# A hybrid encoder kernel: output weights in the order of use, and a spill buffer by half and head

## The chip, the cores and the metric

The kernel runs on one core of one Trainium2 chip. The metric is the device time of one execution in microseconds. Three timed runs of the kernel before lie between 4213.9 and 4220.34 us, with a median of 4215.14 us.

## The reference, cut to what matters

Two sequences (1024 and 2048 tokens, 1024 channels, f32) go through two layers with shared weights. The even layer projects the normed input, runs a state-space mixer (S5, 512 channels) beside a bidirectional RWKV-7 mixer (8 heads of 64 channels), gates both, and puts the concatenation through one output projection. The odd layer is windowed attention with 16 heads of 64, a gate, and an output projection. What the change touches is this:

```python
y = ((y - mean) * lax.rsqrt(var + RW_LN_EPS)).reshape(B, L, RW_WIDTH)   # per head
y = y * rw_ln_g + rw_ln_b
bonus = jnp.sum(rh * kh * rw_r_k, axis=-1, keepdims=True) * vh          # (B, L, 8, 64)
yb = (y + bonus.reshape(B, L, RW_WIDTH)) * jax.nn.silu(z_rw)
x = x + jnp.concatenate([ya, yb], axis=-1) @ ev_w_out                   # 1024 x 1024
...
x = x + (o * jax.nn.silu(z)) @ od_w_out                                 # 1024 x 1024
```

## The kernel before, in words

The program runs in four parts, one after the other. Part one makes S5's inputs. Part two (`input_rkv` with `s5`) projects r, k, v and the low-rank inputs of RWKV and spills them to DRAM. Part three (`mixers`) runs the RWKV recurrence. Part four runs three phases: `even_out` (the even layer's output projection), `odd_in` (the odd layer's input projections) and `attention` (with the odd layer's output projection).

Parts one, two and four are recorded first and then put in order by a planner, class `Program`. `record` notes every operation with a modelled cost and the earlier operations that it depends on. `put` (L414) issues them greedily, by the modelled clocks of the engines and by rank. For a DMA the modelled cost is the bytes of its destination (L378), plus 0.48 us of SP for each issue (L452). A read of an input tensor makes no dependency (L393); a DRAM tile is compared by the address range that it covers (`box`, L343). Each engine then executes its instructions in that fixed order. All DMAs are issued by SP, on one queue. Since the planner replays the recorded operations, nearly every instruction of these parts carries L412 in the profile, so the tile names tell them apart.

RWKV's bonus: `input_rkv` handles the channels in four blocks p of 128 channels, two heads each. It works in segments of 512 tokens, two for the first sequence and four for the second. L820 stores each block's bonus `v` (128 channels on 128 partitions, some hundreds of tokens) into the DRAM tile `bon` of shape [4, 2, 64, L]: block, half, channel in the head, token. There are 24 such stores.

`even_out` works in tiles of 256, 256 and 512 tokens for the first sequence and four times 512 for the second. RWKV's heads are used there in another order: all second halves first, then all first halves. So block b of 128 rows is made of the same half of two neighbouring blocks p. L1810 loads the bonus for block b with the token range of the tile: two runs of 64 rows each. For a tile, `even_out` loads S5's and RWKV's results and gates, normalises RWKV rows (GpSimd, DVE, ScalarE), transposes them on TensorE, and for each b combines them with the bonus and the gate in two DVE operations (L1811, L1812). `emit` (L1769) then splits the block into a high part (ScalarE) and a low part (DVE). TensorE multiplies 8 blocks by the split weights, three products for each (L1724). The tiles `bo` for the bonus have two buffers, shared with a temporary of the normalisation.

The output weights are read by `load_rows` (L1704): eight row blocks of 128 rows, each loaded into a raw tile and split by ScalarE and DVE into a high and a low part. For the even layer (8 loads of 512 KB), the first four blocks are 128 neighbouring rows of `ev_w_out`. The last four follow the order of the heads: two runs of 64 rows (L1743). For the odd layer (`weights`, L1907) there are 8 loads of 256 KB for each of two halves of the columns. All of them are two runs of 64 rows (L1909). `weights(0)` comes at the start of `attention`, and the planner places it beside `odd_in`'s first tile. `weights(1)` comes with the first attention values.

Of the kernel before, what the change touches and what calls it, by code (L numbers as in the profile page):

```python
# [11 lines left out]
F32 = mybir.dt.float32  # L12
# [7 lines left out]
P = 128  # L20
D = 1024
# [449 lines left out]
class Kern:  # L471
# [134 lines left out]
    def spill_tiles(self, dp):  # L606
        self.sp = []
        for s, L in enumerate(self.L):
            t = {}
            t["rk"] = dp.tile([L // P, P, 4, 4, P], F32, name=f"rk{s}")  # L610
            t["v"] = [dp.tile([P, 512], F32, name=f"v{s}_{i}") for i in range(L // P)]
            t["tw"] = dp.tile([64, L], F32, name=f"tw{s}")
            t["bon"] = dp.tile([4, 2, 64, L], F32, name=f"bon{s}")
            t["s5"] = [dp.tile([4, P, 256], F32, name=f"s5{s}_{i}") for i in range(L // 256)]
            t["y"] = [[dp.tile([P, 512], F32, name=f"y{s}_{d}_{i}") for i in range(L // P)] for d in range(2)]
            t["h"] = [dp.tile([min(4, (L - g) // P), P, KT, P], F32, name=f"h{s}_{g}") for g in range(0, L, 512)]
            for n in ("zr", "zs"):
                t[n] = [dp.tile([P, 4, 4, P], F32, name=f"{n}{s}_{i}") for i in range(L // 512)]
            t["x1"] = [dp.tile([P, D], F32, name=f"x1{s}_{i}") for i in range(L // P)]
            t["qkv"] = [dp.tile([P, 2, 1536], F32, name=f"qkv{s}_{i}") for i in range(L // 256)]  # L620
            t["z"] = [dp.tile([P, 8, 512], F32, name=f"z{s}_{i}") for i in range(L // 512)]
            self.sp.append(t)

        nb = [L // 8 for L in self.L]
        self.col = [2, nb[0] + 6]
        for n in ("u", "ys"):
            x = [dp.tile([8, 16, 8, sum(nb) + 8], F32, name=f"{n}_{p}") for p in range(4)]
            for s, t in enumerate(self.sp):
                t[n] = [a[:, :, :, self.col[s]:self.col[s] + nb[s]] for a in x]
            setattr(self, n, x)  # L630
        self.strips = [dp.tile([16, 4, 31, 16], F32, name=f"strip{p}") for p in range(8)]

        self.wsp = [dp.tile([P, 2, KT, P], F32, name=f"wsp{i}") for i in range(13)]
# [64 lines left out]
    def input_rkv(self, st):  # L698
        nc, ins, tc = self.nc, self.ins, self.tc
        W = ins["ev_w_in"][0]  # L700
        cp = st.enter_context(tc.tile_pool(name="p1c", bufs=1))
# [29 lines left out]
        for s, L in enumerate(self.L):  # L731
            t = self.sp[s]
            for t0 in range(0, L, self.seg):
                T = min(self.seg, L - t0)
                last = t0 + T == L
                o0 = t0 - P if t0 else 0
                o1 = L if last else t0 + T - P
# [4 lines left out]
                h = self.stored_T(t["h"], t0, T)  # L742
# [28 lines left out]
                for p in range(4):  # L771
# [3 lines left out]
                    a = o1p.tile([P, SEGW], F32, name="a")[:, :w]  # L775
# [22 lines left out]
                    b = o1p.tile([P, SEGW], F32, name="sq")[:, :w]  # L798
# [4 lines left out]
                    r = o1p.tile([P, SEGW], F32, name="r")[:, :w]  # L803
# [6 lines left out]
                    v = o1p.tile([P, SEGW], F32, name="v")[:, :w]  # L810
# [5 lines left out]
                    for c, n in chunks:  # L816
                        pn = psx.tile([P, 512], F32, name="px")
                        nc.tensor.matmul(pn[:, :n], self.ones2, pb[:, c:c + n], start=True, stop=True)
                        nc.vector.tensor_tensor(v[:, c:c + n], pn[:, :n], v[:, c:c + n], MULT)
                    nc.sync.dma_start(t["bon"][p].rearrange("h r l -> (h r) l")[:, o0:o1], v)  # L820
                for i in range(nt):
                    nc.sync.dma_start(t["v"][o0 // P + i], vt[i])

# [913 lines left out]
    def even_out(self, st):  # L1737
        tc, nc, ins = self.tc, self.nc, self.ins
        cp = st.enter_context(tc.tile_pool(name="eoc", bufs=1))
        wo = ins["ev_w_out"][0]  # L1740

        turned_rows = lambda a: a.rearrange("(b h r) c -> h b r c", h=2, r=64)
        rows = [wo[P * k:P * k + P] for k in range(4)] + [turned_rows(wo[512:D])[1 - b // 2, 2 * (b % 2):2 * (b % 2) + 2] for b in range(4)]  # L1743
        ln = cp.tile([P, 8], F32, name="ln")
        nc.sync.dma_start(ln, ins["rwt_ln"])
        lng, lnb = ln[:, 0:4], ln[:, 4:8]
# [1 line left out]
        lp = st.enter_context(tc.tile_pool(name="eol", bufs=2))  # L1748
# [6 lines left out]
        for s, L in enumerate(self.L):  # L1755
            t = self.sp[s]
            sizes = [self.T1] * (512 // self.T1) if s == 0 else []
            sizes += [512] * (L // 512 - (s == 0))
            for t0, TT in zip(itertools.accumulate([0] + sizes), sizes):
# [9 lines left out]
                def emit(k, m):  # L1769
                    nc.scalar.activation(mh[k], m, AF.Copy)  # L1770
                    nc.vector.tensor_tensor(ml[k], m, f32(mh[k]), SUB)
# [33 lines left out]
                for b in range(4):  # L1805
                    pt = pst.tile([P, 512], F32, name="pt")[:, :TT]
                    for i, y in enumerate(yn):
                        nc.tensor.transpose(pt[:, i * P:(i + 1) * P], y[:, b * P:(b + 1) * P], self.ident)
                    bo = lp.tile([P, 512], F32, name="bo")[:, :TT]
                    nc.sync.dma_start(bo, t["bon"][2 * (b % 2):2 * (b % 2) + 2, 1 - b // 2, :, t0:t0 + TT])  # L1810
                    nc.vector.scalar_tensor_tensor(out=bo, in0=pt, scalar=lng[:, b:b + 1], in1=bo, op0=MULT, op1=ADD)  # L1811
                    nc.vector.scalar_tensor_tensor(out=bo.rearrange("c (i t) -> c i t", t=P), in0=bo.rearrange("c (i t) -> c i t", t=P), scalar=lnb[:, b:b + 1],  # L1812
                                                   in1=zr[:, :, b], op0=ADD, op1=MULT)
                    emit(4 + b, bo)
# [76 lines left out]
    def attention(self, st):  # L1891
        nc, ins, tc = self.nc, self.ins, self.tc
        V, Q = nc.vector, nc.gpsimd
        cp = st.enter_context(tc.tile_pool(name="atc", bufs=1))
# [5 lines left out]
        lp = st.enter_context(tc.tile_pool(name="atl", bufs=2))  # L1900
# [5 lines left out]
        psm = st.enter_context(tc.tile_pool(name="psm", bufs=self.B4, space=PSUM))  # L1906
        def weights(c):  # L1907

            v = ins["od_w_out"][0].rearrange("(k e g r) c -> k g e r c", e=2, g=4, r=64)  # L1909
            rows = [v[b // 4, b % 4] for b in range(8)]  # L1910
            return self.load_rows(cp, lp, [r[:, :, 512 * c:512 * c + 512] for r in rows], f"wo{c}", 0.5, (["wr"], 512, 2))

        w = [weights(0)]
        ring = itertools.cycle(range(16))

# [144 lines left out]
        for j, kv in turn + [(None, None)] * self.LAG:  # L2060
            if j is not None:
                if kv == self.KA and j and j + 2 < len(blocks):
                    keys(j + 2)
                if kv == self.QA and j + 1 < len(blocks):
                    qts[j + 1] = queries(j + 1)
                todo.append(scores(j, kv, qts[j]))
            if len(todo) > self.LAG or j is None:
                x = todo.popleft()
                values(*x)
                if len(w) < 2:  # L2070
                    w.append(weights(1))
                if outs and x[1] == self.OA:
                    d = outs.popleft()
                    out(d, made.pop(d))
                if x[1] == 3:
                    outs.append(x[0])
# [16 lines left out]
    def build(self):  # L2093
        tc = self.tc
        with ExitStack() as root:
# [11 lines left out]


_PLAIN = ["x_prompt", "x_sample", "ev_norm", "ev_w_in", "s5_log_dt", "s5_glu_w", "s5_glu_b", "rw_mu", "rw_w0",
          "rw_w_up", "rw_a0", "rw_a_up", "rw_k_k", "rw_k_a", "rw_r_k", "rw_ln_g", "rw_ln_b", "ev_w_out", "od_norm",  # L2110
          "od_w_in", "at_q_norm", "at_k_norm", "at_sink", "od_w_out"]


def _layout(inputs):
    import numpy as np

    a = {n: np.ascontiguousarray(inputs[n]) for n in _PLAIN}
    g = lambda n, axes, shape: np.ascontiguousarray(np.asarray(inputs[n])[0].transpose(axes).reshape(shape))

    a["ev_w_zr"] = np.ascontiguousarray(np.asarray(inputs["ev_w_in"])[0][:, ZR0:].reshape(D, 4, 2, 64)[:, :, ::-1].transpose(0, 2, 1, 3).reshape(D, 512))  # L2120

    a["od_w_z"] = np.ascontiguousarray(np.asarray(inputs["od_w_in"])[0][:, 1536:].reshape(D, 2, 2, 4, 64).transpose(0, 1, 3, 2, 4).reshape(D, 1024))
    ln = [np.asarray(inputs[n])[0].reshape(2, 2, 2, 64)[:, :, ::-1] for n in ("rw_ln_g", "rw_ln_b")]
    a["rwt_ln"] = np.ascontiguousarray(np.concatenate([x.transpose(1, 3, 2, 0).reshape(P, 4) for x in ln], axis=1))

    for n in ("a_re", "a_im"):
        a["s5t_" + n] = g("s5_" + n, (0, 2, 1), (128, 32))
    for n in ("b_re", "b_im"):
        a["s5t_" + n] = g("s5_" + n, (0, 2, 1, 3), (128, 32, 16))
    for n in ("c_re", "c_im"):  # L2130
        a["s5t_" + n] = g("s5_" + n, (0, 3, 1, 2), (128, 32, 16))
    a["s5t_d"] = np.ascontiguousarray(np.asarray(inputs["s5_d"])[0].reshape(32, 16).T)
    return a
# [14 lines left out]
```

## Time and profile before

| | us |
|---|---|
| median of 3 runs (lowest, highest) | 4215.14 (4213.9, 4220.34) |
| the profiled execution's own time | 4222.45 |
| its span in the trace | 4220.7 |
| TensorE (PE) busy, share of the span | 3795.9, 90% |
| VectorE (DVE) busy | 2819.6, 67% |
| ScalarE (ACT) busy | 1933.0, 46% |
| GpSimd (POOL) busy | 1611.2, 38% |
| mean granted TensorE clock | 0.952 |

The page cuts the span into 40 slices of 105.5 us. A digit is the busy share in tenths; PEclk is the granted TensorE clock in tenths of full speed. `even_out` begins in slice 22 (from 0) and ends in slice 25. There PE shows 6, 6, 8, 8, and the granted clock 7, 7, 8, 9. The slices of `odd_in` that follow show 9 and 9.

The columns of the views below: a stretch of the table by windows has its length, then for PE, PEld (weight loads), DVE, ACT and POOL the busy time with the number of instructions, then the granted clock, the mean busy share of the 16 DMA engines, and GB/s. The chain of waits is followed back from the last instruction: start, length, and what the time went to. "DMA sb<-bon" is the time from a load's issue to the end of the wait for it; "SPq" is time in which SP was issuing.

### The profile page before, as it was taken

The numbers are of one execution on the slowest core, as the hardware profiler recorded it, in microseconds if no ns is written. First come the engines' busy times: TensorE is split into PE (matmuls) and PEld (weight loads), VectorE is DVE, ScalarE is ACT, GpSimd is POOL, SyncE is SP. The second block draws the span as 40 slices with busy tenths as digits, with TensorE's granted clock in tenths as the row PEclk, the third lists the DMA queues.
The fourth block names the chain that finished last, engine by engine and source line by source line (L and its number), as shares of the span: only waits on it lengthen the run. The fifth ranks groups of instructions, "written<-read, shape, count | busy, mean of one in ns | idle before, by whom it ended". The sixth has DMA issues, their size and how long they took to land.

```text
span 4220.7 us, 87574 instructions
## 1 busy us (share of the span) xinstructions
PE 3795.9 (90%) x34128; PEld 3138.8 (74%) x34128; DVE 2819.6 (67%) x5513; ACT 1933.0 (46%) x4807; POOL 1611.2 (38%) x2007
## 2 busy tenths in 40 slices
PE   6878999999899999999996688899999979999999
PEld 4756766676788788888764466789999957878877
DVE  7356655656578888889873565444444449999997
ACT  3334333333345555656653111232333337777776
POOL 4422322222464554555511232122222225555554
PEclk9989999999999999999997789999999989999999
DMA  5576566656533343333443554444444422222221
GB/s 159 148 187 211 163 193 184 182 166 192 176 128 112 112 130 115 109 115 118 122 97 105 179 175 170 167 147 158 155 150 140 143 90 70 76 79 78 78 65 59
DMA packets 530946, 570.30 MB, mean 135 GB/s; under 512 B 92066, under 2 KB 430114, under 8 KB 519268
## 3 DMA queue, kind: packets, MB, share of 16 engines
q1 hardware_dynamic: 530532, 564.71, 43.6%
q8 instruction: 268, 4.39, 0.4%
q14 instruction: 146, 1.20, 0.1%
HBM read 398.03 MB, written 166.56 MB: 134 GB/s over the span
## 4 chain that ended last, share of the span: by engine, by line
PE 51%; DVE 16%; DMA 10%; issue 4%; POOL 3%; ACT 2%; SPq 1%; DVEq 0%; ACTq 0%; POOLq 0%
PE ps L412 36%; DVE sb L412 12%; PE acc L886 5%; DMA sb<-bon 3%; ACT sb L412 2%; PE pc L1332 2%; PE acc L969 2%; DMA sb<-wsp 2%; PE pg L1185 2%; POOL lt L1164 1%; DMA sb<-in_od_w_out 1%; DMA rk<-rk 1%; PE pY L1355 1%; PE pc L1319 1%; PE pc L1310 1%
## 5 line engine op out<-in xcount | busy, mean ns | idle before, releaser
L412 PE MATMUL ps<-sb 128*128 128x512 f32 (+8 forms) x12464 | 2563.8, 360 | 245.1 <-ACT sb L412 115.0
L412 PEld LDWEIGHTS ps<-sb 128*128 128x128 f32 (+2 forms) x12464 | 1975.6, 188 | 656.3 <-ACT sb L412 133.4
L412 POOL TENSOR_TENSOR sb<-sb,sb 128x384 f32<-128x384 f32 (+4 forms) x468 | 470.3, 1022 | 435.8 <-ACT sb L412 242.0
L412 POOL TENSOR_TENSOR sb<-sb 128x512 f32<-128x512 f32 (+5 forms) x358 | 316.4, 888 | 808.2 <-ACT sb L412 337.4
L412 DVE TENSOR_TENSOR sb<-ps,sb 128x512 fp32r<-128x512 f32 (+4 forms) x620 | 401.9, 661 | 226.3 <-PE ps L412 135.4
L412 ACT ACTIVATE sb<-sb 128x4 f32<-128x4 f32 (+7 forms) x352 | 269.4, 768 | 482.8 <-DVE sb L412 162.1
L412 POOL TENSOR_TENSOR sb<-sb,mhalf 128x8 f32<-128x8 f32 (+3 forms) x156 | 221.5, 1421 | 687.1 <-DVE sb L412 685.9
L886 PE MATMUL acc<-h,w 128*128 128x128 f32 x3072 | 450.4, 291 | 14.0 <-DMA w<-in_ev_w_zr 13.1
L886 PEld LDWEIGHTS acc<-h,w 128*128 128x128 f32 x3072 | 385.3, 197 | 39.5 <-POOL rt L1279 13.4
L412 PE MATMUL ps<-ident,sb 128*128 128x128 f32 x1888 | 316.0, 280 | 98.2 <-DVE sb L412 94.9
L412 ACT COPY sb<-ps 128x512 f32<-128x512 f32 (+4 forms) x402 | 194.9, 502 | 433.9 <-PE ps L412 419.3
L412 PEld LDWEIGHTS ps<-ident,sb 128*128 128x128 f32 x1888 | 236.8, 144 | 163.2 <-DVE sb L412 117.4
L412 DVE TENSOR_TENSOR sb<-sb,sb 128x512 fp32r<-128x512 f32 (+6 forms) x219 | 263.3, 1208 | 129.0 <-ACT sb L412 105.0
L412 ACT ACTIVATE sb<-sb,sb 128x384 f32<-128x384 f32 (+3 forms) x486 | 299.3, 619 | 108.8 <-DVE sb L412 58.4
L1164 POOL TENSOR_TENSOR lt<-rk,lb 64x256 f32<-64x256 f32 x288 | 216.2, 759 | 192.8 <-PE pY L1355 82.5
L1324 ACT COPY rt<-pc 32x128 f32<-32x128 f32 x768 | 196.8, 256 | 97.3 <-PE pc L1319 86.1
L412 DVE CUSTOM_DVE_ANT_0 sb<-ps,sb,sb 128x384 f32<-128x384 f32 (+1 forms) x384 | 215.4, 587 | 28.5 <-PE ps L412 25.3
L412 ACT ACTIVATE sb<-ps 128x512 f32<-128x512 f32 x108 | 64.4, 596 | 363.9 <-PE ps L412 355.4
L412 ACT CAST sb<-ps 128x512 fp32r<-128x512 f32 x368 | 202.0, 587 | 60.3 <-PE ps L412 57.5
L1149 POOL TENSOR_TENSOR kb<-rk,f 128x128 f32<-128x128 f32 x384 | 197.8, 547 | 82.5 <-PE pg L1195 68.8
L1339 DVE TENSOR_TENSOR rt<-pc,wc 64x256 f32<-64x256 f32 x376 | 158.3, 421 | 70.0 <-PE pc L1333 35.0
L412 DVE SCALAR_TENSOR_TENSOR sb<-sb,sb 128x512 f32<-128x512 f32 (+5 forms) x154 | 126.1, 826 | 117.0 <-ACT sb L412 112.8
(121 smaller groups left out, 4748.9 us busy)
## 6 DMA issues: line engine op xcount, KB each, us to landing
sb<-wsp SPq DMA_DIRECT2D x65, 1024.0 KB
rk<-rk SPq DMA_DIRECT2D x96, 512.0 KB
sb<-in_od_w_in SPq DMA_DIRECT2D x36, 1024.0 KB
h<-h SPq DMA_DIRECT2D x48, 512.0 KB
sb<-in_od_w_z SPq DMA_DIRECT2D x24, 1024.0 KB
qkv<-sb SPq DMA_DIRECT2D x72, 256.0 KB
sb<-qkv SPq DMA_DIRECT2D x72, 256.0 KB
sb<-in_x_sample SPq DMA_DIRECT2D x32, 512.0 KB
```

The costliest lines, as they stand in the source:

```text
L412: self.ops.append((eng, self.cost(eng, op, outs[-1] if outs[-1] is not k.get("accum_out") else outs[0], ins, a, k), deps, self.rank, lambd ...
L886: nc.tensor.matmul(sums[n][1][:, m * P:m * P + P], w[:, k, m * P:m * P + P], acts[n][0][:, k], start=k == 0, stop=k == KT - 1)
L969: nc.tensor.matmul(ps[:, 256 * (m % 2):256 * (m % 2) + 256], uw_at(k)[:, m], act_at(n)[:, 2 * k:2 * k + 2], start=k == 0, stop=k == 3)
L1149: nc.gpsimd.tensor_tensor(kb[:, sl, :, x, :], arr[n][:, sl, cs], f1[:, sl, cs, a:a + 32], MULT)
L1164: (nc.gpsimd if eng == "POOL" else nc.vector).tensor_tensor(ltv[:, :, :, at:at + 32], arr[n][rows, :, cs], f2[rows, :, cs, off:off + 32], ...
L1185: nc.tensor.matmul(g[64:P, c1, p], kb[0:64, p, c1].rearrange("c s i -> c (s i)"), lt[0:64, c1, 4 + p, 0:64], start=True, stop=True)
L1310: nc.tensor.matmul(pu[32 * q:32 * q + 32, j, :], lt[:, c1, u, 0:32], rt[:, c1, u, :], start=True, stop=True)
L1319: nc.tensor.matmul(pu[rows, 2 + j, :], win["tt"][d][0][rows, sys, :], u1[rows, j, :], start=True, stop=True, tile_position=(32 * q, 32 * q))
L1324: nc.scalar.copy(rt[rows, c1, 2 * q:2 * q + 2, :], pu[rows, 2:4])
L1332: nc.tensor.matmul(pu[0:64, 4 + p, :], lt[:, c1, 4 + p, 64:P], rt[:, c1, 4 + p, :], start=True, stop=True)
L1339: nc.vector.tensor_tensor(nrt[rows, n4 % 2, 4 - 4 * o:8 - 4 * o, :], pu[rows, 4:8], nh["wc"][rows, :, n4:n4 + 1].broadcast_to([64, 4, 64]) ...
L1355: nc.tensor.matmul(pY[32 * q:32 * q + 32, j, :], lt[:, c1, u, 32:64], rt[:, c1, u, :], start=True, stop=True)
```

## The change

The host lays out both output weights in the order in which the kernel reads them (`ev_w_ot`, `od_w_ot`), and passes them in place of `ev_w_out` and `od_w_out`. All loads of weights are then 128 rows at one stride. The DRAM tile `bon` becomes [2, 4, 64, L]: half, block, channel, token. The two runs of 64 rows that a load of the bonus reads then lie one behind the other, and the load is written as 128 rows at one stride of L. The store of one block is no longer contiguous in rows and is cut into two stores of 64 partitions. Sizes, tiles and arithmetic stay.

```diff
-            t["bon"] = dp.tile([4, 2, 64, L], F32, name=f"bon{s}")
+            t["bon"] = dp.tile([2, 4, 64, L], F32, name=f"bon{s}")
...
-                    nc.sync.dma_start(t["bon"][p].rearrange("h r l -> (h r) l")[:, o0:o1], v)
+                    for e in range(2):
+                        nc.sync.dma_start(t["bon"][e, p, :, o0:o1], v[64 * e:64 * e + 64])
...
-        wo = ins["ev_w_out"][0]
-
-        turned_rows = lambda a: a.rearrange("(b h r) c -> h b r c", h=2, r=64)
-        rows = [wo[P * k:P * k + P] for k in range(4)] + [turned_rows(wo[512:D])[1 - b // 2, 2 * (b % 2):2 * (b % 2) + 2] for b in range(4)]
+        rows = [ins["ev_w_ot"][P * k:P * k + P] for k in range(8)]
...
-                    nc.sync.dma_start(bo, t["bon"][2 * (b % 2):2 * (b % 2) + 2, 1 - b // 2, :, t0:t0 + TT])
+                    nc.sync.dma_start(bo, t["bon"][1 - b // 2, 2 * (b % 2):2 * (b % 2) + 2, :, t0:t0 + TT].rearrange("b r l -> (b r) l"))
...
-            v = ins["od_w_out"][0].rearrange("(k e g r) c -> k g e r c", e=2, g=4, r=64)
-            rows = [v[b // 4, b % 4] for b in range(8)]
-            return self.load_rows(cp, lp, [r[:, :, 512 * c:512 * c + 512] for r in rows], f"wo{c}", 0.5, (["wr"], 512, 2))
+            rows = [ins["od_w_ot"][P * b:P * b + P, 512 * c:512 * c + 512] for b in range(8)]
+            return self.load_rows(cp, lp, rows, f"wo{c}", 0.5, (["wr"], 512, 2))
...
+    wo = np.asarray(inputs["ev_w_out"])[0]
+    a["ev_w_ot"] = np.ascontiguousarray(np.concatenate([wo[:512], wo[512:].reshape(4, 2, 64, D).transpose(1, 0, 2, 3)[::-1].reshape(512, D)]))
+    a["od_w_ot"] = np.ascontiguousarray(np.asarray(inputs["od_w_out"])[0].reshape(2, 2, 4, 64, D).transpose(0, 2, 1, 3, 4).reshape(D, D))
```

## Rows read from the trace of the kernel before

**Rows 1.** Busy time by windows: part two, then the stages of part four.
```profile
280.00:1110.00 830.00, 762.13 (x3527) 573.10 (x3525) 510.52 (x729) 301.42 (x665) 237.90 (x238) 0.96 0.61 185
...
2270.00:2355.50 85.50, 22.80 (x80) 17.03 (x80) 26.21 (x45) 13.14 (x20) 13.83 (x25) 0.62 0.43 142
2355.50:2438.40 82.90, 60.44 (x228) 46.01 (x228) 52.26 (x107) 12.63 (x23) 29.53 (x21) 0.85 0.54 176
2438.40:2664.40 226.00, 184.53 (x797) 149.08 (x797) 127.60 (x226) 32.05 (x49) 60.80 (x44) 0.90 0.53 179
2664.40:2792.30 127.90, 114.14 (x754) 105.77 (x754) 54.02 (x77) 35.51 (x48) 32.73 (x27) 0.94 0.45 151
...
3425.90:3472.00 46.10, 16.84 (x88) 14.61 (x88) 17.58 (x44) 18.00 (x49) 15.07 (x21) 0.56 0.24 81
```

**Rows 2.** The chain of waits from 2268 to 2800 us: shares, then pieces.
```profile
by line: PE ps L412 34.7%; DMA sb<-bon 23.1%; DVE sb L412 12.6%; DMA sb<-in_od_w_out 7.5%; DMA sb<-in_ev_w_out 4.5%; SPq L412 3.9%; ACT sb L412 3.6%; issue 3.0%; DMA sb<-x 2.2%; POOL sb L412 2.2%; DMA x<-sb 1.1%; DMA sb<-y 0.9%; DMA y<-ys 0
...
2288.88 16.35 DMA sb<-in_ev_w_out
...
2311.87 9.80 SPq L412
...
2321.77 18.95 DMA sb<-bon
...
2344.19 8.77 DMA sb<-bon
```

**Rows 3.** Busy time by windows: two stretches with few DMA engines, one with all.
```profile
2296.00:2321.00 25.00, 4.38 (x19) 3.00 (x17) 3.91 (x5) 2.50 (x3) 1.64 (x1) 0.67 0.13 53
2428.00:2435.00 7.00, 4.20 (x12) 3.31 (x12) 3.14 (x5) 1.26 (x2) 1.04 (x1) 0.76 0.13 51
...
2482.00:2485.00 3.00, 0.00 (x0) 0.00 (x0) 0.75 (x1) 0.00 (x0) 0.00 (x0) 0.50 1.01 282
```

**Rows 4.** DVE in time: start, length, operation [idle before <- releaser].
```profile
2536.40 1.34 DVE L412 SCALAR_TENSOR_TENSOR sb<-sb 128x128 f32<-128x128 f32 x4 [4.37 <-DMA sb<-zs]
2541.40 0.75 DVE L412 SCALAR_TENSOR_TENSOR sb<-ps,sb,sb 128x512 f32<-128x512 f32 x1 [3.66 <-DMA sb<-bon]
2547.18 0.75 DVE L412 SCALAR_TENSOR_TENSOR sb<-ps,sb,sb 128x512 f32<-128x512 f32 x1 [5.03 <-DMA sb<-bon]
```

**Rows 5.** The whole chain: two pieces of other DMAs, 512 KB and 128 KB.
```profile
1288.12 3.46 DMA rk<-rk
...
2154.75 2.92 DMA s<-z
```

**Rows 6.** DVE in time: the split of one weight block in the first stage.
```profile
2316.38 1.22 DVE L412 SCALAR_TENSOR_TENSOR sb<-sb,sb 128x1024 fp32r<-128x1024 f32 x1 [8.81 <-ACT sb L412]
```

**Rows 7.** SP in time: the issue of both bonus loads of that tile.
```profile
2531.39 1.16 SPq L412 DMA_DIRECT2D sb<-bon  x2
```

**Rows 8.** PE in time, one restart of four.
```profile
2549.37 1.22 PE L412 MATMUL ps<-sb 128*128 128x512 f32 x2 [9.83 <-ACT sb L412]
```

**Rows 9.** Busy time by windows: just after that restart, and a little later.
```profile
2549.40:2553.60 4.20, 4.20 (x10) 2.96 (x11) 3.95 (x7) 1.21 (x2) 0.99 (x1) 0.50 0.74 267
2560.00:2570.00 10.00, 10.00 (x46) 8.28 (x45) 6.32 (x9) 1.26 (x2) 7.58 (x6) 1.00 0.66 207
```

**Rows 10.** The chain of waits from 3400 to 3470 us.
```profile
3422.49 10.04 DMA sb<-in_od_w_out
...
3434.59 9.67 DMA z<-sb
3444.27 6.55 DMA sb<-qkv
```

**Rows 11.** All instructions on `bon`: SP's time, min/median/max in ns; who waited.
```profile
L412 SPq DMA_DIRECT2D sb<-bon x28: 482/504/1318, 2288.3 to 2648.5; - x28
L412 SPq DMA_DIRECT2D bon<-sb x24: 319/332/469, 300.4 to 1107.6; - x24
...
  DVE sb L412: 72.7, 16
```

More of the change, by code (lines that the diff above doesn't have):

```diff
@@ L2109 @@
 _PLAIN = ["x_prompt", "x_sample", "ev_norm", "ev_w_in", "s5_log_dt", "s5_glu_w", "s5_glu_b", "rw_mu", "rw_w0",
-          "rw_w_up", "rw_a0", "rw_a_up", "rw_k_k", "rw_k_a", "rw_r_k", "rw_ln_g", "rw_ln_b", "ev_w_out", "od_norm",
-          "od_w_in", "at_q_norm", "at_k_norm", "at_sink", "od_w_out"]
+          "rw_w_up", "rw_a0", "rw_a_up", "rw_k_k", "rw_k_a", "rw_r_k", "rw_ln_g", "rw_ln_b", "od_norm",
+          "od_w_in", "at_q_norm", "at_k_norm", "at_sink"]
 def _layout(inputs):
```

## The prediction

> **What bounds the kernel now.** I read the page first. Over the span TensorE is busy for 90%, and the slices of `even_out` fall well below that, together with the granted clock. So I cut part four into stages with the table by windows [rows 1]. Column three is the busy time of PE, so the idle time of a stage is its length less that: 62.7 us in the first stage (85.5 less 22.8; it ends where TensorE gets the last product blocks of the first tile), 22.5 in the second (tiles one and two), 41.5 in the third (five tiles of 512 tokens, four restarts), 13.8 in the fourth (the end of `even_out` and `odd_in`'s first tile), 29.3 in the last (attention's start). That is 169.8 us. The clock column shows 0.62, 0.85, 0.90, 0.94 and 0.56 in the idle stages: part of the work after each idle time runs at the lower level of 1.2 GHz.
>
> Then I asked the chain of waits what those stages wait for [rows 2]. Of 532 us, 23.1% (123 us) go to loads of the bonus, 7.5% (40 us) to `od_w_out`, 4.5% to `ev_w_out`, and SP needs 3.9% for issuing, 9.8 us of it in one piece. The reader is to see that a 128 KB or 256 KB load costs 9 to 19 us.
>
> Why so long is in the DMA columns [rows 3]. Where only two-run loads are under way, the busy share of the DMA engines is 0.13 and the rate 51 to 53 GB/s, for 4 KB rows (from 2296) as for 2 KB rows (from 2428). 0.13 of 16 engines is two engines: one for each run of 64. Where loads of 128 rows at one stride follow one another (`y`, from 2482) the share is 1.01 and the rate 282 GB/s. Two bonus loads issued together don't use four engines: the second one releases DVE 5.78 us after the first (2541.40 and 2547.18) [rows 4], and 256 KB at 51 GB/s are 5.1 us. So both sit on the same two engines, one behind the other, and every other load is late by its sixteenth shares on these two.
>
> **The change, part by part.** Each number is against the profiled execution (4222.45 us; span 4220.7); the median of the three runs is 7.3 us below it, and I carry the saving over to the median as it is.
>
> *What a load costs afterwards.* No row shows a bonus load over all engines. A piece of 128 KB takes 2.92 us in the chain from issue to release, one of 512 KB 3.46 us [rows 5]; for 256 KB or 128 KB with little ahead I take 2.9. Bounds: 2.9 at best, and with several MB ahead in the queue the load waits for these as now; I price that per stage.
>
> *First stage.* In the chain, the fifth weight block goes from 16.35 to 2.9 (13.4 saved), the 9.80 us in which SP could not issue shrink to an ordinary issue of 0.4 (9.4), and two bonus pieces of 18.95 and 8.77 go to 2.9 each (16.0 and 5.9) [rows 2]: 44.8 us. What is late next is DVE: the splits of the later weight blocks (1.22 each [rows 6]) ran in the long waits and now stand one behind the other, two of them bare in the chain. 44.8 less some 2.8 gives **42**. It cannot exceed the 62.7 us of idle time; the lower bound, if the other loads of the stage (gates, S5, `x`) take the place, I put at half, 21.
>
> *Second stage.* Idle 22.5; I leave 6 of it for `y` and the normalisation. At a mean clock of 0.85, 30% of 82.9 us (25 us) lay at the lower level; taking half of that as work, some 6 us come back. 22.5 - 6 + 6 = **22** (between 10 and 28).
>
> *Third stage.* In a steady tile DVE waits 4.37 us for the gate `zs` (its four operations start at 2536.40), then 3.66 and 5.03 us for bonus three and four [rows 4]. Both bonus loads are issued from 2531.39 on [rows 7], 5 us before `zs` lands, so they will be there when DVE is through with `zs` (2536.40 + 1.34). TensorE restarts 2.19 us after DVE starts on bonus four, at 2549.37 after 9.83 us of idle [rows 8]: its own queue ended at 2539.54. DVE starts on bonus three at 2537.7, on four at 2538.4, and TensorE restarts at 2540.6: 1.1 us idle. Four restarts keep about 5 of 41.5 us. After a restart 10 products take 4.2 us at a granted clock of 0.50, later 46 take 10 us at 1.00 [rows 9]: 10 products are 2.2 us then, so each restart gives back 2.0 us if the clock no longer falls, 8 in all. 41.5 - 5 + 8 = 44.5; I take **43** (between 22 and 45).
>
> *Fourth stage.* The chain has 40 us of `od_w_out` and 12 of `x` behind it, but TensorE idles only 13.8: the rest lies beside products. Of these some 4 remain, and the clock (0.94) returns 2 or 3: **12** (6 to 17).
>
> *Attention's start.* Pieces of 10.04, 9.67 (a store of `z` that stands behind two weight loads) and 6.55 [rows 10] go to 2.9 each: 26.3 - 8.7 = **17.6**. The work in the stage is short operations between engines; I count nothing for the clock (12 to 22).
>
> *What costs nothing.* The order of part four stays: the planner prices a DMA by its destination's bytes and asks no dependency of inputs, and `bon` is only read there. Each load keeps its size, count and place; SP's time on a bonus load falls from 0.50 to about 0.33 us.
>
> *The stores.* 24 stores become 48 of 64 partitions each. SP's time for one is 0.33 us [rows 11], so 8 us are added over 830 us of part two; queued behind the second store are SP's next issues, 0.33 us later. Only DVE is named as waiting on `bon` at all, 72.7 us in 16 waits, all behind the loads. So the cost is 0 while nobody waits. But the planner sees 24 more issues, and its greedy order of part two can change on every engine. PE idles 68 us there: an order cannot gain more than that, and I put the loss at no more than the same. I take 0, nearest to the 8 us of SP's time, with ±10 in the range.
>
> The Trainium skill speaks against these stores: "DMA: Bandwidth & Descriptors", section "Rules for kernel authors", advises one transfer of 128 partitions in place of two on the halves, since the halves share the same engines. By the fixed part of some 2 us that the same page fits for DMAs issued by GpSimd ("Anatomy of one DMA"), an estimate for 24 more, each waited for, is 48 us. The trace shows no wait behind a bonus store in the rows above, so the sum keeps 0.
>
> **Sum.** 42 + 22 + 43 + 12 + 17.6 = 136.6, taken as 137. 4222.45 - 137 = 4085 for a profiled execution, and 4215 - 137 = **4078 us** for the median.
>
> **The rivals.**
> *A. The next loads take the place.* `zs` (4.37 us before the bonus in a steady tile) and `y` become the last to land, and half the idle time stays. For it: the stages move 142 to 179 GB/s already and will move the same bytes in less time. Against it: 282 GB/s in the stretch with all engines. Stages near their lower bounds, at 21, 10, 26, 8 and 15: 80 saved, 4215 - 80 = 4135.
> *B. More returns than I count.* The two engines are a drag on every other load too, and the clock stays up. Stages at 52, 28, 45, 17 and 22: 164, 4051.
> *C. The stores are waited for.* A store pair costs one more landing. With the 2.92 us of rows 5 for each of 24: 70 us, 4215 - 137 + 70 = 4148. Against it: no one waits for the stores now.
> *D. The loads don't widen*, because the view of two blocks is still carried as two runs of 64. Then nothing moves: 4215. Against it: the two dimensions have one common stride, L, and the weights have no second dimension left.
> *E. Slower: a worse order of part two.* Place: 280 to 1110 us. The planner's counts for SP shift by 24 issues and every later choice may fall differently. It decides from the point at which that part loses more than the 137 us saved later, so that its idle time of 68 us triples; losing 160 gives 4238. For it: greedy orders are touchy. Against it: 8 us of SP's time in 830, and each store follows the last operation on its block.
>
> **How the numbers follow.** Forecast 0.69 (100 to 155 saved: 4060 to 4115), A 0.14, B 0.10, C 0.02, D 0.02, E 0.03. From the middle the range goes to B's 4051 less some 10 for the order of part two on one side, and to A's 4135 less a few on the other: 4042 to 4130 leaves out A's far end, C, D and E. This kernel's measurement cannot tell 0.2% (8.4 us) from no change. Faster by more: 0.69 + 0.14 + 0.10 + 0.02 = 0.95; the same: D, 0.02; slower: E, 0.03.
>
> **What will show it.** Stage lengths of about 43, 61, 183, 116 and 28 us in place of 85.5, 82.9, 226, 127.9 and 46.1, counted between the same operations; part two within 10 us of 830. No stretch in part four at a DMA share of 0.13. DVE's waits for `bon` fall from 72.7 to under 10 us, SP's median time on a bonus load from 504 to near 330 ns. A restart in the steady tiles has about 1 us of idle time before it and a granted clock of 1.00 after it. Stretches at 0.13 would say that the loads have not widened (D). Wide loads, but idle restarts whose releaser is `zs`, `y` or `x`, would say A. Bonus waits gone and the time still unmoved would mean that I read the wrong wait as the last one.

## The result, and the profile after

The changed kernel took 4068.49 us (median of 4 runs, 4061.76 to 4070.05), the kernel before beside it 4217.74 us (4213.9 to 4223.13). The ratio is 0.9642 [0.9625, 0.9659]: 149 us less. The profiled execution took 4070.05 us, with a span of 4068.3 us and a mean granted clock of 0.971 (before 0.952).

The table by windows of the changed kernel answers to [rows 1]. The stages are cut at the same products, counted from the end, and the columns are the same. The first line is part two; it starts a few products later than in [rows 1], and its fellow of before stands with the experiments.

```profile
300.70:1110.80 810.10, 733.34 (x3438) 554.53 (x3437) 500.70 (x733) 299.42 (x674) 240.28 (x256) 0.96 0.62 186
...
2266.60:2308.40 41.80, 21.87 (x80) 16.66 (x80) 25.92 (x45) 12.81 (x20) 15.98 (x25) 0.72 0.84 288
2308.40:2372.00 63.60, 54.91 (x229) 42.24 (x229) 52.13 (x108) 12.64 (x23) 27.68 (x21) 0.95 0.68 230
2372.00:2555.60 183.60, 176.20 (x797) 143.27 (x797) 124.43 (x227) 32.06 (x50) 67.26 (x44) 1.00 0.63 220
2555.60:2662.10 106.50, 106.11 (x754) 99.83 (x755) 54.07 (x77) 35.62 (x49) 32.00 (x27) 1.00 0.57 190
...
3295.70:3323.20 27.50, 14.46 (x87) 12.19 (x88) 16.50 (x43) 16.63 (x46) 14.89 (x21) 0.69 0.34 111
```

Read it against [rows 1] as length less PE's busy time. The five stages idle 19.9, 8.7, 7.4, 0.4 and 13.0 us, 49.4 in all where they idled 169.8. The same products also keep PE busy for 25 us less (22.80, 60.44, 184.53, 114.14, 16.84 against 21.87, 54.91, 176.20, 106.11, 14.46), since the clock column rose to 0.72, 0.95, 1.00, 1.00 and 0.69. 120 us of idle time and 25 us of slow products are the 145 us that these stages gave. The DMA share rose in every stage. Rate times length gives 12.0, 14.6 and 40.4 MB in the first three stages, against 12.1, 14.6 and 40.5 before: the same bytes went through in less time.

The instructions on `bon` in the changed kernel (operation, count, SP's time as min/median/max in ns; last, who waited) answer to [rows 11]:

```profile
L412 SPq DMA_DIRECT2D bon<-sb x48: 479/525/1884, 297.0 to 1096.9; - x48
L412 SPq DMA_DIRECT2D sb<-bon x28: 319/320/664, 2284.8 to 2546.9; - x28
...
  DVE sb L412: 5.5, 4
```

DVE's waits for the bonus fell from 72.7 us in 16 waits to 5.5 us in 4. A load costs SP 320 ns, where it cost 504. The 48 half stores cost 525 ns each, where 24 whole ones cost 332: by these medians some 25.2 us of SP's time in place of 8.0.

The chain of waits of the changed kernel from 2265 to 2665 us (shares, then pieces) answers to [rows 2], and covers the same work in 400 us that [rows 2] covers in 532:

```profile
by line: PE ps L412 54.1%; DVE sb L412 15.6%; DMA sb<-zs 7.3%; DMA sb<-bon 4.8%; issue 4.2%; POOL sb L412 3.8%; ACT sb L412 3.1%; DMA sb<-y 2.5%; SPq L412 1.4%; DMA x<-sb 1.4%; DMA sb<-in_at_sink 0.8%; DMA y<-ys 0.4%; SPq L1369 0.3%; PE pY 
...
2270.52 1.23 SPq L412
...
2298.91 6.04 DMA sb<-zs
...
2322.21 7.19 DMA sb<-zs
...
2399.56 8.29 DMA sb<-zs
...
2451.81 6.11 DMA sb<-bon
...
2499.01 6.80 DMA sb<-bon
```

The output weights are gone from it, the bonus went from 23.1% (123 us) to 4.8% (19 us), and products lead it. A load of the gate `zs` is the longest transfer now. SP no longer stands in an issue: in [rows 2] one took 9.80 us, and the longest from the end of the recurrence to 3323 us now takes 1.2 us. The bonus pieces that are left last 6 to 7 us: these loads are issued while `zs` is still under way.

DVE in time, in one steady tile (start, length, operation, idle before and its releaser), answers to [rows 4]:

```profile
2455.14 1.36 DVE L412 SCALAR_TENSOR_TENSOR sb<-sb 128x128 f32<-128x128 f32 x4 [3.35 <-DMA sb<-zs]
2456.39 0.77 DVE L412 SCALAR_TENSOR_TENSOR sb<-ps,sb,sb 128x512 f32<-128x512 f32 x1
2458.02 0.75 DVE L412 SCALAR_TENSOR_TENSOR sb<-ps,sb,sb 128x512 f32<-128x512 f32 x1 [0.87 <-DMA sb<-bon]
```

PE's restarts in these tiles answer to [rows 8]:

```profile
2412.06 1.88 PE L412 MATMUL ps<-sb 128*128 128x512 f32 x7 [1.31 <-ACT sb L412]
...
2460.21 32.73 PE L412 MATMUL ps<-sb 128*128 128x512 f32 x143 [0.92 <-ACT sb L412]
2508.10 32.75 PE L412 MATMUL ps<-sb 128*128 128x512 f32 x143 [1.63 <-ACT sb L412]
2555.60 32.74 PE L412 MATMUL ps<-sb 128*128 128x512 f32 x143 [1.22 <-ACT sb L412]
```

The wait for `zs` is still there (4.37 us before, 3.35 now). Behind it bonus three costs no wait and bonus four 0.87 us, where they cost 3.66 and 5.03. TensorE restarts 2.19 us after DVE starts on bonus four, as it did before, but after 0.9 to 1.6 us of idle time and not 9.83. In three of the four, the 143 products of a tile then run in one piece of 32.7 us, at the full clock (34.8 us after the restart of [rows 8]).

### The profile page after: what moved, and what is told of

Its sections match the earlier page's. It is cut to its first block, busy times and chain, and to the rows that moved or that the text cites. A ratio compares the mean times of both kernels' runs of the same rounds, so it can differ in the third digit from the quotient of the medians.

```text
span 4068.3 us, 87603 instructions
## 1 busy us (share of the span) xinstructions
PE 3756.4 (92%) x34128; PEld 3112.1 (76%) x34128; DVE 2815.9 (69%) x5513; ACT 1932.0 (47%) x4807; POOL 1620.1 (40%) x2007
## 4 chain that ended last, share of the span: by engine, by line
PE 46%; DVE 16%; DMA 4%; issue 3%; POOL 3%; ACT 2%; SPq 1%; DVEq 0%; POOLq 0%; ACTq 0%
PE ps L412 30%; DVE sb L412 11%; PE acc L887 5%; PE pc L1333 2%; PE pg L1186 2%; ACT sb L412 2%; PE acc L970 2%; DMA rk<-rk 1%; PE pc L1320 1%; PE pY L1356 1%; POOL lt L1165 1%; PE pc L1311 1%; DVE ng L1251 1%; DVE z L1253 1%; DVE lt L1206 1%
## 5 line engine op out<-in xcount | busy, mean ns | idle before, releaser
L412 PE MATMUL ps<-sb 128*128 128x512 f32 (+8 forms) x12464 | 2530.8, 358 | 163.9 <-ACT sb L412 56.7
L412 PEld LDWEIGHTS ps<-sb 128*128 128x128 f32 (+2 forms) x12464 | 1955.0, 186 | 562.9 <-DVE sb L412 101.5
L412 POOL TENSOR_TENSOR sb<-sb 128x512 f32<-128x512 f32 (+5 forms) x358 | 329.0, 923 | 713.1 <-ACT sb L412 322.5
L412 ACT CAST sb<-ps 128x512 fp32r<-128x512 f32 x368 | 202.0, 587 | 57.1 <-PE ps L412 54.4
L412 DVE TENSOR_SCALAR sb<-sb,sb 128x384 f32<-128x384 f32 (+4 forms) x264 | 190.3, 750 | 18.1 <-POOL sb L412 16.1
```

The lines of the kernel that those rows point to most:

```text
L412: self.ops.append((eng, self.cost(eng, op, outs[-1] if outs[-1] is not k.get("accum_out") else outs[0], ins, a, k), deps, self.rank, lambd ...
```

## The experiments

The theory: a load of two runs of 64 rows is carried by two DMA engines, one of 128 rows at one stride by all of them, and nothing else in the change matters. Its rivals: it is the layout in memory and not the number of runs; or it is the order of part two that comes with the doubled stores. I give the time that each kernel saved in a stage against the kernel before, in us, cut at the same products of one profiled execution each; the first stage counts from its first product. Part two's column is its length, which was 820.3 before.

| kernel | part two | first | second | third | fourth | attention's start |
|---|---|---|---|---|---|---|
| forecast | | 42 | 22 | 43 | 12 | 17.6 |
| changed kernel | 810.1 | 43.6 | 19.4 | 42.4 | 21.3 | 18.7 |
| two_runs_kept | 810.5 | 0.3 | -0.2 | 1.7 | 0.4 | -0.2 |
| stores_only | 810.9 | 1.3 | -1.4 | -4.0 | 0.5 | -0.2 |
| weights_only | 820.2 | 37.3 | -0.7 | -2.3 | 18.8 | 17.0 |
| bonus_only | 813.6 | 8.8 | 22.1 | 35.3 | 1.1 | 0.2 |
| halves_apart | 816.0 | 39.5 | 16.2 | 36.7 | 19.7 | 17.4 |
| weights_relaid_bonus_halves | 816.9 | 42.8 | 16.0 | 34.1 | 21.3 | 17.7 |
| four_runs | 822.6 | 24.5 | 9.2 | 21.4 | 19.8 | 10.2 |

In part four every engine executes the same operations in the same order in all these kernels but the two whose loads are cut in halves, so the other rows differ there by their transfers alone. The rows of two_runs_kept and stores_only, which save nothing, show how far one execution scatters: up to 2 us in most stages, 4 in the third.

**two_runs_kept.** All of the change, its layout, its 48 stores and its order; but one row of padding stands behind every 64 rows, so that each load is again two runs.

```diff
-            t["bon"] = dp.tile([2, 4, 64, L], F32, name=f"bon{s}")
+            t["bon"] = dp.tile([2, 4, 1, 65, L], F32, name=f"bon{s}")
...
-            rows = [ins["od_w_ot"][P * b:P * b + P, 512 * c:512 * c + 512] for b in range(8)]
+            rows = [ins["od_w_pad"][2 * b:2 * b + 2, :64, 512 * c:512 * c + 512] for b in range(8)]
```

> The changed kernel with one spare row behind every 64 rows of the bonus and of the split weight blocks in DRAM, so that each load is two runs of 64 rows again; same rows, same sizes, same count of loads and stores. Width theory (a load of two runs occupies two DMA engines, and that alone made the kernel before slow): part four goes back to what it was, about 145 us more than the changed kernel, 4205 to 4220 us, stretches with a DMA share of 0.13, DVE waits some 70 us for the bonus. Layout theory (it helps that the rows lie one behind the other in DRAM): 4065 to 4080 us.

It took 4219.31 us, ratio 0.9982 [0.997, 0.9994]. Part four saved nothing. The table by windows, in the first stage, has the columns of [rows 1], and below it stand its instructions on `bon`:

```profile
2300.00:2310.00 10.00, 0.69 (x2) 0.29 (x2) 1.83 (x2) 1.06 (x1) 0.00 (x0) 0.50 0.13 52
```

```profile
L412 SPq DMA_DIRECT2D sb<-bon x28: 488/504/1382, 2278.2 to 2634.9; - x28
...
  DVE sb L412: 71.6, 17
```

The share of 0.13 and the 52 GB/s of [rows 3] are back, and so are 504 ns on SP and 71.6 us of waiting. The layout alone does nothing; the number of runs decides.

**stores_only.** The kernel before, with each bonus store cut in two; the layout and all loads stay.

```diff
-                    nc.sync.dma_start(t["bon"][p].rearrange("h r l -> (h r) l")[:, o0:o1], v)
+                    for e in range(2):
+                        nc.sync.dma_start(t["bon"][p, e, :, o0:o1], v[64 * e:64 * e + 64])
```

> The kernel before with its 24 bonus stores cut into 48 of 64 partitions, at the same addresses; all loads as before. Order theory: part two takes the order of the changed kernel and ends about 10 us earlier, the recurrence gives most of it back, part four is as before: 4205 to 4217 us. Waited-for stores (24 more landings of 2.9 us): 4285. If the stores cost nothing and the shift was chance: 4217.

4219.36 us, ratio 0.9987 [0.9976, 0.9997]: no cost, so rival C fell. Part four, with two-run loads as before, saved nothing. Both intervals, of two_runs_kept and of this kernel, end just below 1; that is looked at below.

**weights_only** and **bonus_only.** Each part of the change alone: the first is the changed kernel with the three lines on `bon` put back, the second the kernel before with these three lines alone.

```diff
-            t["bon"] = dp.tile([2, 4, 64, L], F32, name=f"bon{s}")
+            t["bon"] = dp.tile([4, 2, 64, L], F32, name=f"bon{s}")
...
```

```diff
-            t["bon"] = dp.tile([4, 2, 64, L], F32, name=f"bon{s}")
+            t["bon"] = dp.tile([2, 4, 64, L], F32, name=f"bon{s}")
...
```

> Only the weights are laid out; the bonus as before. Width theory with the sum by stages: the first stage saves some 35 us (weight blocks and SP's blocked issues, and the bonus no longer behind them), attention's start 18, the fourth stage 21, the second and third stages nothing, part two nothing: 4135 to 4150 us. If the weights were hidden and the bonus the whole cost: 4215.

> Only the bonus is laid out by half and head, with 48 stores; the weights as before. Width theory: second and third stage save 19 and 42 us as in the changed kernel, the first little (5 to 10, the bonus still stands behind weight blocks), the fourth and attention's start nothing, part two about 4: 4135 to 4150 us. The two halves add up to the whole 149 if neither hides behind the other. If they hide behind each other, each alone gives less than 50.

They took 4153.93 us, ratio 0.9831 [0.9817, 0.9846], and 4146.3 us, ratio 0.9809 [0.9791, 0.9827]; the first lies 4 us beyond what was expected. In the table the weights give the first and fourth stage and attention's start, the bonus the second and third and part of the first; the two rows add up to the changed kernel within 3 us in four stages and to 9 us less in the third. There weights_only's -2.3 lies within the scatter; the rest is bonus_only's, with 11.2 us idle and 179.5 us of products against 7.4 and 176.2, and why is open. What is left waiting shows in the lists of waiters: first DVE for `bon` in weights_only (us, times), then ScalarE for the even layer's weights and for the odd layer's in bonus_only. These are 61.7, 35.4 and 58.2 us, where the changed kernel has 5.5, 4.6 and 6.8.

```profile
  DVE sb L412: 61.7, 16
```

```profile
  ACT sb L412: 35.4, 4
```

```profile
  ACT sb L412: 58.2, 11
```

**halves_apart.** The kernel before in its old layout, each load of two runs issued as two loads of 64 rows.

```diff
-            nc.sync.dma_start(raw, r)
+            if len(r.shape) == 3:
+                for e in range(2):
+                    nc.sync.dma_start(raw[64 * e:64 * e + 64], r[e])
+            else:
+                nc.sync.dma_start(raw, r)
...
-                    nc.sync.dma_start(bo, t["bon"][2 * (b % 2):2 * (b % 2) + 2, 1 - b // 2, :, t0:t0 + TT])
+                    for e in range(2):
+                        nc.sync.dma_start(bo[64 * e:64 * e + 64], t["bon"][2 * (b % 2) + e, 1 - b // 2, :, t0:t0 + TT])
```

> The kernel before, layouts untouched, each load of two runs written as two loads of 64 rows, one for each run and half of the partitions. Width theory: both halves use all engines, so the saving of the changed kernel comes without a new layout, less the issues: some 56 more SP issues of 0.33 us and a new order of part four: 4065 to 4095 us. Layout theory (scattered runs are slow in themselves): 4205 to 4225.

4093.03 us, ratio 0.9698 [0.9679, 0.9717]. Without any new layout, most of the gain is there, for 48 more issues in part four (the expectation had 56). The instructions on `bon`, and the table by windows while half loads of weights and bonus are under way (eight are issued from 2293.8 to 2299.5):

```profile
L412 SPq DMA_DIRECT2D sb<-bon x56: 444/588/746, 2294.3 to 2568.6; - x56
...
  DVE sb L412: 9.3, 6
```

```profile
2296.00:2300.00 4.00, 4.00 (x20) 3.25 (x19) 3.56 (x5) 1.06 (x1) 2.50 (x3) 1.00 0.94 221
```

**weights_relaid_bonus_halves.** The changed kernel's weights; the bonus in its old layout with 24 stores, each load cut in two as above.

> Both weights laid out in the order of use as in the changed kernel; the bonus buffer keeps its old layout and its 24 stores, and each bonus load is cut into two loads of 64 rows (56 issues). Width theory: all engines carry every load, so the four weight terms are those of the changed kernel (some 43, 19, 21 and 18 us), and the five tiles of 512 tokens save what they saved with the halves apart (36.7 against 42.4 us), because SP spends some 1.1 us on a block's two issues in place of 0.32. Sum 137 to 142 saved, 4075 to 4090. Rival, that the new order of part two which the 24 extra stores bring is worth the 9 us by which the profiles differ ahead of part four: 4085 to 4098. Rival, that the layout itself matters and not the number of engines: the third stage keeps its 226 us, 4105 to 4115.

4087.28 us, ratio 0.9674 [0.9644, 0.9705]. That excludes the layout (4105 to 4115), but lies in the width theory's range and in that of the rival on part two's order, so it does not tell these two apart. By the ratios it is 0.3% above the changed kernel, with intervals that overlap. Part two is 6.8 us longer in the table; PE's restarts show another part:

```profile
2469.35 1.36 PE L412 MATMUL ps<-sb 128*128 128x512 f32 x4 [2.11 <-ACT sb L412]
...
2521.86 35.81 PE L412 MATMUL ps<-sb 128*128 128x512 f32 x143 [2.53 <-ACT sb L412]
2573.96 32.75 PE L412 MATMUL ps<-sb 128*128 128x512 f32 x143 [2.76 <-ACT sb L412]
```

The idle time is 2.1 to 2.8 us before these three (0.63 in the tile ahead of them), against 0.9 to 1.6 us, and one tile's 143 products take 35.81 us in place of 32.75. Over the second and third stage the profiles differ by 12 us. The expectation's reason was SP, which spends 587 ns on a half load; no run takes that apart from the later landing of `zs`.

**four_runs.** As two_runs_kept, with a row of padding behind every 32 rows: each load is four runs, each bonus block four stores (96).

```diff
-            t["bon"] = dp.tile([2, 4, 64, L], F32, name=f"bon{s}")
+            t["bon"] = dp.tile([2, 4, 2, 33, L], F32, name=f"bon{s}")
...
-            rows = [ins["od_w_ot"][P * b:P * b + P, 512 * c:512 * c + 512] for b in range(8)]
+            rows = [ins["od_w_pad"][4 * b:4 * b + 4, :32, 512 * c:512 * c + 512] for b in range(8)]
```

> As two_runs_kept, but with a spare row behind every 32 rows: each load is four runs of 32 rows, the bonus is stored by 96 stores of 32 partitions. Width theory, engines in proportion to the runs: four engines, so 256 KB at some 102 GB/s take 2.6 us and 512 KB 5.1 us, half of what two runs take; stretches with a DMA share of 0.25. First stage some 10 us longer than the changed kernel, third stage 3 us more at each of four restarts and some clock, fourth 3 and attention's start 5: 4090 to 4125 us. If any number of runs under 16 ends on two engines: 4205 to 4225. If only two runs are special: 4065 to 4080.

4143.31 us, ratio 0.9809 [0.9783, 0.9835]: between two engines and all, though 18 us above the expected range. The table by windows behind a bonus load and four weight loads of this kind, a restart of PE, the instructions on `bon`, and two issues of SP:

```profile
2305.00:2309.00 4.00, 2.47 (x11) 1.69 (x10) 1.84 (x3) 1.06 (x1) 1.64 (x1) 1.00 0.25 103
```

```profile
2508.75 35.33 PE L412 MATMUL ps<-sb 128*128 128x512 f32 x143 [5.21 <-ACT sb L412]
```

```profile
L412 SPq DMA_DIRECT2D bon<-sb x96: 303/419/3346, 300.0 to 1112.7; - x96
...
  DVE sb L412: 39.7, 14
```

```profile
2304.03 4.48 SPq L412 DMA_DIRECT2D sb<-y  x1
...
2309.69 5.19 SPq L412 DMA_DIRECT2D sb<-y  x1
```

0.25 of 16 engines is four, and 103 GB/s is twice 51 to 53. That is the theory's dose: two, four and all engines give 71.6, 39.7 and 5.5 us of DVE's waiting, restarts after 9.8, 5.2 and 1.2 us, and 9.80, 5.19 and 1.2 us for an issue that SP stands in. I had put the price of four runs too low: at half of the waits, the idle time of a restart is still long enough that the products after it start at the lower level of the clock (35.33 us for 143 products). The Trainium skill states this rule ("DMA: Bandwidth & Descriptors", section "Why a DMA increments its semaphore by 16 and not by 1"): a copy goes to the largest number of engines up to 16 that divides the outermost dimension on both sides. The traces agree, with 0.13 for two runs and 0.25 for four.

**after_weights_earlier** and **after_weights_first.** Is there more to be had by loading the even layer's weights sooner? The changed kernel, with their place in the recording moved ahead (`T1, WP = 256, 2` becomes `256, 1` and `256, 0`).

> The changed kernel with the even layer's weight loads recorded before RWKV's part of the first tile in place of behind it. In the changed kernel TensorE still idles 17 us before its first product of part four, with the DMA engines at 288 GB/s. If the order of the loads is the cause, the first product comes up to 5 us earlier: 4060 to 4068 us. If the bytes are the cause, or the later loads of y and the bonus then come last: 4065 to 4080.

> The changed kernel with the even layer's weight loads recorded before everything of the first tile. The first product also needs S5's rows and gate, which then stand behind up to four blocks of weights (2 MB at 288 GB/s, 7 us): 4068 to 4080 us, slower than after_weights_earlier. If the weights were what is late, 4058 to 4066.

4071.21 us, ratio 0.9651 [0.9629, 0.9672], and 4073.79 us, ratio 0.9651 [0.9631, 0.9671]: no gain. From the last product of the recurrence to the end of the first stage took 43.3 us in the changed kernel, 48.8 and 53.4 us in these two. The second and third stage gave it back (22.5 and 46.1, 27.7 and 46.9 us saved). No version here beats the changed kernel.

**What the store order does.** The table's column for part two falls into two groups. Kernels with 48 stores need 810.1, 810.5, 810.9 and 813.6 us, the last two kernels above 810.9 and 809.5; kernels with 24 need 816.0, 816.9, 820.2 and 820.3. Part two of the kernel before and of stores_only, by windows:

```profile
300.36:1120.70 820.34, 743.17 (x3437) 558.12 (x3437) 501.14 (x733) 300.11 (x674) 237.65 (x254) 0.95 0.60 184
```

```profile
307.15:1118.05 810.90, 733.67 (x3437) 554.11 (x3437) 501.84 (x734) 299.69 (x674) 239.59 (x256) 0.96 0.62 185
```

The idle time is the same (77.2 and 77.2 us); the same products take 9.5 us less. The kernels with 48 stores all execute one new order of part two (up to its end, at least 758 of TensorE's 4432 places hold another product), those with 24 the old one. Four executions of the old order scatter by 4.3 us and six of the new one by 4.1, so the new order with its stores is some 7 us faster on average, by how its products run and not by a wait. four_runs, with 96 stores and a third order, needs 822.6 us. The two kernels that save nothing in part four lie at 0.9982 and 0.9987, which is 8 and 5 us of 4223 (the medians differ by 4) and points the same way, with 1 just outside the intervals. Part of the 9.5 us is the clock: of TensorE's busy time in part two, 59.2 us lie at the lower level before and 48.0 in stores_only; such work takes half as long at the full clock, so half of the difference, 5.6 us, is the clock's. In this the two orders overlap (50.7 to 62.0 us and 46.0 to 57.1). With half of that time taken off, the products take 711.4 to 714.2 us in the old order and 708.9 to 710.1 in the new one. Why these last few us go, and whether by the order or by the cut stores, no run here shows.

## Why the prediction was right, step by step

The forecast of 4078 us (137 saved) stood against 4068.49 us (149 saved), and the mechanism is the one it named. The two profiles differ by 152.4 us where the sum had 136.6. Of the 15.8 us more, 8.8 lie in the five stages, all of it in the fourth, and 3.5 each ahead of part four and behind attention's start.

*Two engines for two runs.* Shown by two_runs_kept (0.13 again, nothing saved) and four_runs (0.25, part of it saved); that a plain cut of the same loads works too (halves_apart) excludes the layout. Cut into windows of 2 us, the five stages of the kernel before have 62 of 284 at 0.12 to 0.14 and 47 to 55 GB/s, those of the changed kernel none, and rival D fell.

*First, second, third stage, attention's start.* 42, 22, 43 and 17.6 us were forecast and 43.6, 19.4, 42.4 and 18.7 measured. The idle time left was put at 20.7, 6 and 5 us and is 19.9, 8.7 and 7.4. The clock was to give 6 and 8 us in the second and third stage, and PE's busy time fell by 5.5 and 8.3. The split of the first stage between its causes was not as priced: 22.8 us for weights and SP's blocked issue, 21.9 for two bonus pieces, less 2.8. Alone, the weights give 37.3 and the bonus 8.8, so most of what stood as bonus in that chain went with the weights ahead of it. At attention's start one transfer is left in the chain, where three stood in [rows 10]:

```profile
3300.10 3.10 DMA sb<-qkv
```

*The steady tile.* The restart stood where it was worked out, but not for the whole reason. I had priced a bonus load at 2.9 us from [rows 5], whose 3.46 us for 512 KB is the shortest of ten such pieces of `rk` in that chain (the longest is 6.89), and expected both to have landed by the time that DVE is through with `zs`; the pieces in the chain last 6.1 to 6.8 us, and bonus four comes 0.87 us late. It cost little, because these loads run beside the wait for `zs`. What is late next is `zs`, as rival A had it, but with 7.3% of the chain, and not with half of the idle time.

*Fourth stage: the term that was mis-sized.* 12 us were forecast, with a bound of 17; it was 21.3. Idle time fell from 13.8 to 0.4 us (I left 4). And the clock gave 8.0 us, not 2 or 3: I had read the mean of 0.94 as little, without cutting the stage. Cut, the kernel before shows three stretches at a low clock, one after the last restart of the kind of [rows 8], two after shorter idle times in `odd_in`'s first tile:

```profile
2664.00:2672.00 8.00, 7.57 (x23) 6.00 (x23) 4.47 (x9) 3.20 (x6) 1.10 (x2) 0.65 0.44 151
2743.00:2748.00 5.00, 4.31 (x24) 4.32 (x25) 1.32 (x2) 0.00 (x0) 2.34 (x2) 0.67 0.23 77
2760.00:2772.00 12.00, 9.41 (x56) 9.24 (x57) 4.74 (x6) 1.75 (x3) 3.85 (x2) 0.72 0.50 164
```

With two levels, 1.00 and 0.50, these means say that 5.6, 3.3 and 6.7 us lay at the lower one, 15.6 us. TensorE was busy in some 14.2 us of that time, and this work takes half as long at the full clock: 7.1 us, against 8.0 measured. A mean of 0.94 over 128 us hides 15 us at half speed; that sum was there to be made.

*The stores.* Forecast at 0 with ±10. SP's price was too low (525 ns a half store, so 17 us more and not 8), but nobody waits for it, and with it came an order of part two that is 9 to 10 us shorter in the profiles of stores_only and two_runs_kept. Here the Trainium skill's advice against two transfers on the halves of the partitions ("DMA: Bandwidth & Descriptors", section "Rules for kernel authors") did not bear on the time: the cut stores cost SP more and the kernel nothing. For the loads the case is the other way round, since one load of two runs uses two engines and its two halves use all (halves_apart).

*What stays open.* The recurrence, which the change does not touch, took 1147.8 us before and 1154.3 us after in these two profiles, and between 1146.2 and 1156.8 us in the others, with no relation to the edits that I can see. That is why the profiles differ by 3.5 us at the start of part four, where part two alone gives 10.

## What to carry to other kernels

Look at the DMA share where a slow load is alone: here a share of 2/16 or 4/16 was the number of runs in its view, and another layout or a plain cut into loads of one stride brought all engines back. Where a restart's idle time goes, add half of the time that the products behind it ran at the lower clock, found by cutting the stage into short windows and not from its mean. An edit that changes the number of issues also changes a greedy order elsewhere: time that part in a kernel with the edit alone, and more than once, since one order of part two scattered by 4 us.

## What the runs showed of the hardware

SP needs 320 ns to issue a bonus load of 128 rows at one stride and 504 ns for two runs, but 525 ns for a store from 64 partitions and 588 ns for a load into 64 (halves_apart), where a store from 128 takes 332. Two engines (a share of 0.13) carry 51 to 53 GB/s, four (0.25) 103. While two-run weight loads are under way, SP stands 9.80 us in the issue of one load behind them, with four runs 4.48 and 5.19 us.
